# Four compressed rows between the rows of a pair, low parts on VectorE, and fewer rows scaled on ScalarE

## The chip, the core and the metric

The kernel runs on one core of a Trainium2 chip. The metric is the device time of one execution in microseconds, the median of several runs. The core has TensorE (matrix products, with its own queue for weight loads), VectorE (DVE in the rows), ScalarE (ACT), GpSimd (POOL) and SyncE (SP), which issues the transfers. Each engine works through its own queue in order and waits at semaphores for the others.

## What is computed

A transformer layer on 512 rows of width 1024, in float32: a normalisation modulated by a condition vector, a projection, two kinds of attention, an output projection, a second normalisation and a gated feed-forward part with a causal convolution. The change touches only the attention. Cut to that:

```
qa, ka, va, qb, kc, vc, ksl, vsl, kw, vw, gl = split(u @ w_in)
o_a = dilated_attention(rope(qa), rope(ka), va)               # 8 heads, 3 patterns in one masked softmax
kcc, vcc = compress(kc), compress(vc)                         # 512 positions -> 31 blocks, small gelu nets
for each of 8 heads of qb (2 groups of 4):
    o = g0 * softmax(q kcc') vcc + g1 * attention over (ksl, vsl) + g2 * attention over (kw, vw)
y = concat(o_a, o_b) @ w_o
```

The gates g come from a sigmoid of gl. With 512 rows and 8 selectable blocks of 64, all blocks are selected, so the second and the third part of o are causal attention over all keys before the row.

## The kernel before

Products keep float32 accuracy by splitting: each operand is a high part, rounded to the matrix format by a ScalarE copy, and a low part, the difference, taken on VectorE or GpSimd. A product is three matmuls (`mm3`, lines 259 to 261).

The attention is a list of 76 rows, numbered from 0. A row is one head with one kind of keys and one or two query tiles of 128 positions: (0, 1), (2) or (3), three rows for a head and kind. `BH(i)` gives the twelve rows of pair i of the gated heads (two heads, two kinds of keys), `AH(j)` the six rows of pair j of the dilated ones; `cmp_row(t)` gives one of the four compressed rows: all eight heads against the 31 compressed keys for query tile t. The constant `ROWS` sets the order: pairs b0 (rows 0 to 11), b1 (12 to 23), a0, a1 (24 to 35), b2 (36 to 47), the compressed rows 'c' (48 to 51), b3 (52 to 63), a2, a3 (64 to 75).

A loop over k (line 1303 on) interleaves the steps of several rows by the string `SEQ`: in step k it emits the scores of row k+1 (TensorE, L707 and L708; L645 for a compressed row), the masking and the row minimum of row k (VectorE, L715), its exponential (ScalarE, L721), the scaling of row k-1, the transposes of row k-3 ("turn", L741), the high part (ScalarE, L760) and the low part (VectorE, L764) of what was turned, and the product with the values of row k-5 (L789). Scaling is done by VectorE's reciprocal (L726) and then, where `e['act']` is set, by a gate multiplication on VectorE (L730) and one ScalarE activation per tile (L732), and otherwise by one GpSimd instruction per tile that takes the gate as a second scalar (L736). The flag is set for rows 4 to 19 (line 1297).

Between these steps the loop calls the filling products, two, three or four per row by the row's width: the projections of the other heads, cut into 256 pieces. Their weights come in groups, `quad_chunks(i, post)`: index 0 to 3 for the values and the second query group, 4 to 7 for the pairs a0 to a3. The high parts of a chunk are made on ScalarE (L1122), the low parts on VectorE for i under 6 and on GpSimd for a2 and a3 (L1125), two instructions of 128x512 for a chunk. Behind a finished group its results are copied, rotated (`rotate`, GpSimd, L424 to L427) and split; `v_split` does the splitting of values with one ScalarE copy and two VectorE subtractions (L505, L506). Further work that is started and then called once at a time, four times a step, are the small compression nets (`hidden`: additions L519 on GpSimd, products L1160; first the keys, then the values), the reductions for the modulation (L1033, VectorE) and the folding of finished heads. A compressed row's seven VectorE steps stand at L652 to L655, L662 to L664 and its last two subtractions at L682; its scores wait for the compressed keys and values (`needing`). After the last compressed row and the last row of a pair, `after` starts `cmp_end(h)`, which adds the compressed part to the pair's sum.

A planner places the instructions: within an engine the order follows the order of emission where it can, and later work is drawn forward into gaps that the planner's own cost model sees. Its gaps need not be those of the chip.

Of the kernel before, what the change touches and what calls it, by code (L numbers as in the profile page):

```python
# [106 lines left out]
def body(ctx, tc, nc, a, out, dbg=None):  # L107
# [18 lines left out]
    PS = 2  # L126
# [27 lines left out]
    SEQ = 'mtsmawcpmmfru'  # L154
    CUTS = (512,)
    OP = (16, 8, 0)
    ROWS = ('b0', 'b1', 'a0', 'a1', 'b2', 'c', 'b3', 'a2', 'a3')
    ORDER = ('vb', 'va0', 'a0', 'a1', 'qb23', 'va1', 'a2', 'a3')
    NBP = 1
    N0P = ()  # L160
# [2 lines left out]
    CD = ()  # L163
# [3 lines left out]
    V, A, P, T = nc.vector, nc.scalar, nc.gpsimd, nc.tensor  # L167
# [23 lines left out]
    def q4(name, dt=F32, shape=(128, 1024)):  # L191
        return slot('q4', NQ, list(shape), dt, name)
# [4 lines left out]
    def wraw(shape=(128, 1024)):  # L197
        return slot('wr', NR, list(shape), F32, 'wraw')
# [4 lines left out]
    def whl(shape=(128, 1024)):  # L203
        return slot('wh', 2, list(shape), F32R, 'whi'), slot('wl', 2, list(shape), F32R, 'wlo')
# [31 lines left out]
    def f(x):  # L236
        return x.bitcast(F32)

    def load(dst, src, queue=nc.sync):
        queue.dma_start(dst, src)  # L240
# [76 lines left out]
    for t in range(NT):  # L317
# [3 lines left out]
        y = xt[t]  # L321
        ag = stats(y)
        if True:
            nb = offset_of(ag, P if NBP else V)
            cs = [slice(0, 1024)]
            if t == 3:
                cs = [slice(0, X3), slice(X3, 1024)]
                if XV:
                    c = cs.pop(0)
# [38 lines left out]
    for j in range(KD):  # L368
        if j == 0:
            ada_cols(0)  # L370
        w = wraw((128, NC1))
        load(w, a['w_first'][j])
        wh, wl = whl((128, NC1))
# [5 lines left out]
        y = xT[j]  # L379
# [49 lines left out]
    def product(w, ts, banks):  # L429

        wh, wl = w
        for t in range(NT):
            tk = slice(128 * t, 128 * t + 128)
            if len(banks) <= t // 2:
                while live[0] >= BANKS['acc']:
                    count('acc')
                    run_misc(True)
                banks.append(acc_bank('quad'))
            o_ = banks[t // 2][:, 256 * (t % 2):256 * (t % 2) + 256]
            for i, k in enumerate(ts):  # L440
                mm3(o_, uh[k][:, tk], ul[k][:, tk], wh[:, i, :], wl[:, i, :],
                    k == 0 and t % 2 == 0, k == KD - 1 and t % 2 == 1)
                yield
# [57 lines left out]
    def v_split(dst, src, n):  # L501
        s4 = src.rearrange("p (n e d) -> p n e d", e=2, d=64)
        d4 = dst.rearrange("p (n s d) -> p n s d", s=4, d=64)
        A.activation(d4[:, :, 0:4:3, :], s4, AF.Copy)
        V.tensor_sub(d4[:, :, 1, :], s4[:, :, 0, :], f(d4[:, :, 0, :]))  # L505
        V.tensor_sub(d4[:, :, 2, :], s4[:, :, 1, :], f(d4[:, :, 3, :]))  # L506


    def blocks_of(src, eng, res):
# [42 lines left out]
    for b in (1, 0):  # L552
        y = q4('yc', F32, (128, 2, 4, 64))
# [338 lines left out]
    def cmp_end(h):  # L892

        yield from acc_wait()
        pv = acc_bank('pvc')
        cmp_mm(h, pv, True)
        yield 2
        V.tensor_add(ysum[h], ysum[h], pv)
        acc_done()
        yield 1  # L900
        yield from pair_split(h)
# [170 lines left out]
    def count(x):  # L1072
        counts[x] += 1
# [4 lines left out]
    def start_misc(gen, early=False):  # L1078
        misc.insert(0 if early else len(misc), [0, gen])

    def run_misc(forced=False):

        tick[0] += 1
        for m in sorted(misc, key=lambda m: m[0]) if forced else list(misc):
            if forced or m[0] <= tick[0]:
                d = next(m[1], -1)
                if d == -1:
                    misc.remove(m)
                    continue
                if d == 'wait':  # L1090
                    m[0] = tick[0] + 1
                    continue
                m[0] = tick[0] + (d or 1)
                return
# [9 lines left out]
    def finish(post):  # L1104
        yield from post
        quads[1] += 1

    def quad_chunks(i, post):
        st = {}

        def fetch(c):
            def run():
                st['w', c] = wraw((128, 4, 256))
                load(st['w', c], a['w_quad'][i][:, 4 * c:4 * c + 4, :])
            return run

        def prep(c):
            def run():
                w = st['w', c]
                wh, wl = whl((128, 4, 256))  # L1120
                for p in range(2):
                    A.activation(wh[:, 2 * p:2 * p + 2], w[:, 2 * p:2 * p + 2], AF.Copy)  # L1122
                    yield
                for p in range(0, 4, PS):
                    (V if i < 6 else P).tensor_sub(wl[:, p:p + PS], w[:, p:p + PS], f(wh[:, p:p + PS]))  # L1125
                    yield
                st[c] = wh, wl
                yield
            return run

        def go(c):
            def run():
                while c not in st:
                    count('prep')
                    run_misc(True)
                if c == 0:
                    st['b'] = []
                    while quads[1] < quads[0] - 1:
                        count('post')
                        run_misc(True)  # L1140
                    quads[0] += 1
                yield from product(st[c], range(4 * c, 4 * c + 4), st['b'])
                if c == 1:
                    start_misc(finish(post(st['b'])))
            return run
        return [(fetch(c), prep(c), go(c)) for c in range(2)]
# [90 lines left out]
    def needing(names, e):  # L1237
        go = e['scores']

        def scores():  # L1240
            need(*names)
            go()
        return dict(e, scores=scores)

    BH = lambda h: [r for e in range(2) for typ in range(2) for r in nsa(h, e, typ)]
    AH = lambda j: [r for e in range(2) for r in a_head(j, e)]
    cmp_rows = [needing(('qb23', 'kc', 'vc'), cmp_row(t)) for t in range(NT)]

    def after(row, *hs):
        go = row['use']  # L1250

        def use():
            go()
            for h in hs:
                start_misc(cmp_end(h))
        row['use'] = use

    rows, done_b = [], []
    for r in ROWS:
        if r == 'c':  # L1260
            rows += cmp_rows
            after(rows[-1], *[h for h in done_b if h not in CD])
        else:
            i = int(r[1])
            rows += (BH if r[0] == 'b' else AH)(i)
            if r[0] == 'b':
                if 'c' in ROWS[:ROWS.index(r)] and i not in CD:
                    after(rows[-1], i)
                done_b.append(i)


    early = {}
# [21 lines left out]
        start_misc(late_steps(GAP, st_))  # L1294
    nrow = len(rows)
    for k, r in enumerate(rows):
        r['act'] = 4 <= k < 20
    rows[0]['scores']()
    wo_started = [False]
    wo_fill = wo_first()  # L1300
# [210 lines left out]
    def down_weights(k, hi, lo):  # L1511
        w = wraw()
        load(w, a['w_down'][k])
        P.tensor_mul(w, w, g2)  # L1514
        return w
# [11 lines left out]
    for k in range(KF - NL):  # L1527
        w = down_weights(k, None, None)
        wh, wl = whl()
# [8 lines left out]
    for t in range(NT):  # L1538
# [3 lines left out]
        for c0, c1 in zip(edges, edges[1:]):  # L1542
            h, cs = c0 // 512, slice(c0 % 512, (c1 - 1) % 512 + 1)
# [18 lines left out]
```

## Time and profile before

| what | value |
| --- | --- |
| median of three runs | 721.15 us (719.63 to 722.5) |
| the profiled execution | 724.09 us, span 722.3 us, mean granted clock 0.988 |
| TensorE busy | 692.0 us, 96% of the span |
| VectorE busy | 459.2 us, 64% |
| ScalarE busy | 347.3 us, 48% |
| GpSimd busy | 238.7 us, 33% |

In busy times of a stretch the number in brackets is how many instructions started there. The granted clock is a share of TensorE's full 2.4 GHz. In a timeline the first number is the start, the second the time taken, and a bracket at the end is the engine's idle time just before, with the instruction that ended it. A row's state tile `sa__` carries a running number, so the same number on VectorE, ScalarE and GpSimd is the same row (`sa__1128` is row 4, `sa__2478` row 31, `sa__2520` row 32, `sa__2706` row 37).

### The profile page before, as it was taken

The page shows a single profiled execution, that of the slowest core. Times are in us where ns is not written, and L with a number is a line of the kernel's source. Part 1 is how long each engine was busy: PE and PEld are TensorE (multiplying, and loading weights), DVE is VectorE, ACT ScalarE, POOL GpSimd, SP SyncE. Part 2 cuts the span into 40 slices and gives each one's busy share as a digit, 9 for nine tenths or more (in the row PEclk, how much of TensorE's full clock was granted, in tenths as well). Part 3 has the DMA queues.
Part 4 walks back from the last instruction along what each step waited for, and adds up shares of the span by engine and source line. Part 5 has one row for each costly group of instructions (what it writes and reads, how often), then busy time and mean ns, then how long its engine had stood idle before and what let it go on. Part 6 is the DMA issues. An engine that isn't in the chain of part 4 may idle for free.

```text
span 722.3 us, 10901 instructions
## 1 busy us (share of the span) xinstructions
PE 692.0 (96%) x3964; PEld 598.6 (83%) x3964; DVE 459.2 (64%) x965; ACT 347.3 (48%) x706; POOL 238.7 (33%) x252
## 2 busy tenths in 40 slices
PE   8999899899989998999999999999999999999995
PEld 7999689897889886778898888888888788888884
DVE  7879877767886989978844444554543363445236
ACT  5657487744567588916553333333433341232101
POOL 2002510342466484512310110111110355765326
PEclk8999999999999999999999999999999999999999
DMA  9967741256451212350112233444423233434002
GB/s 343 386 207 197 208 144 68 59 204 234 146 204 60 59 61 87 130 192 1 59 59 88 88 100 133 142 147 148 146 91 114 88 110 123 139 123 136 10 15 102
DMA packets 31069, 93.07 MB, mean 129 GB/s; under 512 B 4132, under 2 KB 4900, under 8 KB 31016
## 3 DMA queue, kind: packets, MB, share of 16 engines
q1 hardware_dynamic: 30580, 92.20, 37.8%
q8 instruction: 31, 0.51, 0.3%
q10 hardware_dynamic: 436, 0.18, 0.1%
q14 instruction: 22, 0.18, 0.1%
HBM read 87.13 MB, written 2.10 MB: 124 GB/s over the span
## 4 chain that ended last, share of the span: by engine, by line
PE 75%; DVE 11%; ACT 5%; POOL 3%; issue 3%; DMA 2%; POOLq 0%; SPq 0%; DVEq 0%; ACTq 0%
PE d L261 6%; PE d L260 6%; PE d L259 6%; PE pvv L259 5%; PE pvv L261 5%; PE pvv L260 5%; PE pg L259 5%; PE pg L261 5%; PE pg L260 5%; PE first L393 3%; PE quad L259 3%; PE quad L260 2%; PE quad L261 2%; PE pT L741 2%; PE hid L1160 2%
## 5 line engine op out<-in xcount | busy, mean ns | idle before, releaser
L256 DVE TENSOR_TENSOR wlo<-wraw,whi 128x1024 fp32r<-128x1024 f32 x60 | 83.7, 1395 | 122.6 <-ACT whi L255 121.4
L255 ACT ACTIVATE whi<-wraw 128x1024 fp32r<-128x1024 f32 x60 | 63.6, 1060 | 139.9 <-PE pg L260 68.1
L259 PE MATMUL quad<-whi,u 128*128 128x256 f32 x256 | 75.8, 296 | 1.0 <-DVE qo L471 1.0
L260 PE MATMUL quad<-wlo,u 128*128 128x256 f32 x256 | 73.1, 286 | 0.0
L261 PE MATMUL quad<-whi,u 128*128 128x256 f32 x256 | 73.0, 285 | 0.0
L1514 POOL TENSOR_TENSOR wraw<-wraw,arow 128x1024 f32<-128x1024 f32 x22 | 58.9, 2688 | 37.0 <-DMA wraw<-w_down 35.8
L259 PE MATMUL pg<-u,whi 128*128 128x512 f32 (+1 forms) x176 | 67.7, 385 | 0.0
L260 PE MATMUL pg<-u,whi 128*128 128x512 f32 (+1 forms) x176 | 66.8, 380 | 0.0
L261 PE MATMUL pg<-u,wlo 128*128 128x512 f32 (+1 forms) x176 | 66.8, 379 | 0.0
L261 PE MATMUL pvv<-u,wlo 128*128 128x512 f32 (+1 forms) x176 | 66.8, 379 | 0.0
L259 PE MATMUL pvv<-u,whi 128*128 128x512 f32 (+1 forms) x176 | 66.8, 379 | 0.0
L260 PE MATMUL pvv<-u,whi 128*128 128x512 f32 (+1 forms) x176 | 66.8, 379 | 0.0
L256 POOL TENSOR_TENSOR hl<-cv,hh 128x512 fp32r<-128x512 f32 x14 | 23.8, 1704 | 110.6 <-ACT hh L255 110.6
L259 PEld LDWEIGHTS quad<-whi,u 128*128 128x128 f32 x256 | 49.5, 193 | 5.8 <-issue 3.9
L260 PEld LDWEIGHTS quad<-wlo,u 128*128 128x128 f32 x256 | 49.5, 193 | 1.1 <-issue 0.4
L715 DVE CUSTOM_DVE_ANT_0 p<-sp,masks 128x128 f32<-128x128 f32 (+1 forms) x96 | 44.6, 482 | 8.6 <-PE sp L708 8.2
L261 PEld LDWEIGHTS quad<-whi,u 128*128 128x128 f32 x256 | 49.5, 193 | 0.1
L741 PE MATMUL pT<-ident,p 128*128 128x128 f32 x240 | 39.9, 280 | 7.4 <-POOL p L736 4.1
L260 PEld LDWEIGHTS pg<-u,whi 128*128 128x128 f32 x176 | 33.1, 188 | 6.7 <-issue 0.5
L259 PEld LDWEIGHTS pg<-u,whi 128*128 128x128 f32 x176 | 33.1, 188 | 6.5 <-issue 0.5
L261 PEld LDWEIGHTS pg<-u,wlo 128*128 128x128 f32 x176 | 33.1, 188 | 6.3
L260 PEld LDWEIGHTS pvv<-u,whi 128*128 128x128 f32 x176 | 33.1, 188 | 6.2
(650 smaller groups left out, 1855.3 us busy)
## 6 DMA issues: line engine op xcount, KB each, us to landing
wraw<-w_up SPq DMA_DIRECT2D x44, 512.0 KB, 3.2
wraw<-w_down SPq DMA_DIRECT2D x22, 512.0 KB, 3.3
ada<-ada_col SPq DMA_DIRECT2D x32, 256.0 KB, 5.8
wraw<-w_quad SPq DMA_DIRECT2D x16, 512.0 KB, 4.3
wraw<-ada_col SPq DMA_DIRECT2D x16, 512.0 KB, 4.3
wraw<-ada_row SPq DMA_DIRECT2D x16, 512.0 KB, 3.3
x<-x SPq DMA_DIRECT2D x8, 512.0 KB, 4.9
wraw<-w_o SPq DMA_DIRECT2D x8, 512.0 KB, 3.2
```

The source lines that it names most:

```text
L255: A.activation(hi, raw, AF.Copy)
L256: lo_engine.tensor_sub(lo, raw, f(hi))
L259: T.matmul(o_, sh, mh, start=start, stop=False)
L260: T.matmul(o_, sh, ml, start=False, stop=False)
L261: T.matmul(o_, sl, mh, start=False, stop=stop)
L393: T.matmul(o_, l[:, tk], r[:, cs], start=(j == 0 and t % 2 == 0 and x == 0 and term is terms[0]), stop=(j == KD - 1 and t % 2 == 1 and x = ...
L715: V.tensor_tensor_reduce(p[:, cols[i]], e['s'][:, cols[i]], masks[:, m0:mask0 + 512], 1.0, 3e38, op0=ALU.add, op1=ALU.min, accum_out=m_[:, ...
L741: T.transpose(e['t'][:, 128 * j:128 * j + 128], e['p'][:, 128 * j:128 * j + 128], ident)
L1160: T.matmul(acc[0:62, 0:256], bl[l_ // 8][:, l_ % 8, :], w[:, l, :], start=l_ == 0, stop=l_ == 15)
L1514: P.tensor_mul(w, w, g2)
```

## The change

The compressed rows no longer stand as a block behind pair b2. One is put behind each of its groups of three rows, so that in the new numbering they are rows 39, 43, 47 and 51, and b2 takes the others from 36 to 50; from row 52 on nothing moves. `cmp_end` of b0, b1 and b2 still starts after the last compressed row. The low parts of the weight groups a2 and a3 are taken on VectorE like the others (eight instructions). The flag for scaling on ScalarE is set for rows 12 to 19 only; rows 4 to 11, all of pair b0, are scaled on GpSimd. `v_split` makes its two subtractions in one instruction over both halves (it is called twelve times).

```
-    ROWS = ('b0', 'b1', 'a0', 'a1', 'b2', 'c', 'b3', 'a2', 'a3')
+    ROWS = ('b0', 'b1', 'a0', 'a1', 'b2', 'b3', 'a2', 'a3')
+    AT = (('b2', 2), ('b2', 5), ('b2', 8), ('b2', 11))
...
-        V.tensor_sub(d4[:, :, 1, :], s4[:, :, 0, :], f(d4[:, :, 0, :]))
-        V.tensor_sub(d4[:, :, 2, :], s4[:, :, 1, :], f(d4[:, :, 3, :]))
+        V.tensor_sub(d4[:, :, 1:3, :], s4, f(d4[:, :, 0:4:3, :]))
...
-                    (V if i < 6 else P).tensor_sub(wl[:, p:p + PS], w[:, p:p + PS], f(wh[:, p:p + PS]))
+                    V.tensor_sub(wl[:, p:p + PS], w[:, p:p + PS], f(wh[:, p:p + PS]))
...
-    rows, done_b = [], []
+    rows, last = [], {}
     for r in ROWS:
-        if r == 'c':
-            rows += cmp_rows
-            after(rows[-1], *[h for h in done_b if h not in CD])
-        else:
-            i = int(r[1])
-            rows += (BH if r[0] == 'b' else AH)(i)
-            if r[0] == 'b':
-                if 'c' in ROWS[:ROWS.index(r)] and i not in CD:
-                    after(rows[-1], i)
-                done_b.append(i)
+        i = int(r[1])
+        new = (BH if r[0] == 'b' else AH)(i)
+        for n_, row in enumerate(new):
+            rows.append(row)
+            if (r, n_) in AT:
+                rows.append(cmp_rows[AT.index((r, n_))])
+        if r[0] == 'b':
+            last[i] = new[-1]
+    for i, row in last.items():
+        after(max(row, cmp_rows[-1], key=lambda x: [y is x for y in rows].index(True)), i)
...
-        r['act'] = 4 <= k < 20
+        r['act'] = 12 <= k < 20
```

## Rows read from the trace of the kernel before

**Rows 1.** The page's first part: busy us, share of the span, instructions.
```profile
PE 692.0 (96%) x3964; PEld 598.6 (83%) x3964; DVE 459.2 (64%) x965; ACT 347.3 (48%) x706; POOL 238.7 (33%) x252
```

**Rows 2.** Busy us by stretch; behind the engines the granted clock, DMA share, GB/s.
```profile
80.00:100.00 20.00, 17.57 (x118) 14.31 (x118) 17.45 (x57) 13.79 (x37) 10.41 (x11) 1.00 0.62 210
100.00:120.00 20.00, 20.00 (x143) 16.95 (x142) 13.31 (x48) 15.57 (x42) 0.00 (x0) 1.00 0.26 86
200.00:220.00 20.00, 17.68 (x134) 17.36 (x134) 16.71 (x55) 12.90 (x36) 14.30 (x17) 0.91 0.54 191
212.00:252.00 40.00, 38.47 (x320) 37.51 (x319) 31.75 (x98) 26.73 (x70) 23.46 (x35) 1.00 0.23 75
220.00:240.00 20.00, 20.00 (x169) 19.76 (x168) 13.00 (x39) 13.98 (x36) 12.84 (x21) 1.00 0.08 30
240.00:260.00 20.00, 18.47 (x145) 17.34 (x144) 19.45 (x64) 13.45 (x39) 8.47 (x12) 1.00 0.21 55
```

**Rows 3.** Timeline of TensorE: three waits (start, us taken, instruction, idle before).
```profile
90.50 0.55 PE L741 MATMUL pT<-ident,p 128*128 128x128 f32 x3 [1.08 <-ACT p L732]
...
203.33 0.89 PE L741 MATMUL pT<-ident,p 128*128 128x128 f32 x4 [2.32 <-POOL p L736]
...
247.75 0.39 PE L259 MATMUL quad<-whi,u 128*128 128x256 f32 x1 [1.00 <-DVE qo L471]
```

**Rows 4.** Timeline of GpSimd, 195 to 205 us.
```profile
195.99 2.14 POOL L736 TENSOR_SCALAR p<-p,sa__2478 128x384 f32<-128x384 f32 x1 [0.36 <-DVE sa__2478 L726]
198.13 3.51 POOL L1125 TENSOR_TENSOR wlo<-wraw,whi 128x512 fp32r<-128x512 f32 x2
201.61 1.66 POOL L736 TENSOR_SCALAR p<-p,sa__2520 128x512 f32<-128x512 f32 x1
...
204.05 0.59 POOL L736 TENSOR_SCALAR p<-p,sa__2594 128x384 f32<-128x384 f32 x1
```

**Rows 5.** Busy us by stretch as in rows 2, around the wait for GpSimd.
```profile
202.00:204.00 2.00, 0.67 (x5) 0.68 (x5) 1.97 (x7) 0.36 (x2) 2.00 (x3) 0.90 0.66 217
204.00:206.00 2.00, 2.00 (x12) 2.00 (x11) 1.72 (x3) 0.60 (x1) 0.64 (x2) 0.50 0.91 334
206.00:208.00 2.00, 2.00 (x14) 2.00 (x14) 1.33 (x6) 0.97 (x3) 0.00 (x0) 0.74 0.69 250
```

**Rows 6.** Line 1125: ns shortest/median/longest, first and last start in us.
```profile
L1125 DVE TENSOR_TENSOR wlo<-wraw,whi x24: 628/688/989, 52.9 to 180.9; 128x512 fp32r<-128x512 f32 x24
...
L1125 POOL TENSOR_TENSOR wlo<-wraw,whi x8: 1269/1288/2262, 198.1 to 240.7; 128x512 fp32r<-128x512 f32 x8
```

**Rows 7.** Timelines of GpSimd, VectorE and ScalarE around row 4.
```profile
84.83 8.84 POOL L519 TENSOR_TENSOR bst<-vct,cin 64x248 f32<-64x248 f32 x8
...
87.19 0.15 DVE L726 RECIPROCAL sa__1128<-sa__1128 128x1 f32<-128x1 f32 x1
...
89.06 0.68 DVE L730 TENSOR_TENSOR sa__1128<-sa__1128,gates 128x1 f32<-128x1 f32 x1
...
89.83 0.62 ACT L732 ACTIVATE p<-p,sa__1128 128x384 f32<-128x384 f32 x1 [1.31 <-DVE sa__1128 L730]
```

**Rows 8.** Timeline of GpSimd: scaling with a gate (x2 is one wide row).
```profile
212.09 0.98 POOL L736 TENSOR_SCALAR p<-p,sa__2677,gates 128x128 f32<-128x128 f32 x2
213.72 0.66 POOL L736 TENSOR_SCALAR p<-p,sa__2706,gates 128x384 f32<-128x384 f32 x1 [0.65 <-PE quad L261]
...
217.46 0.77 POOL L736 TENSOR_SCALAR p<-p,sa__2744,gates 128x512 f32<-128x512 f32 x1
```

**Rows 9.** Single tiles (columns as in rows 6): compressed scores, their masking, compressed values, split values.
```profile
L645 PE MATMUL sc<-kcs,qe x16: 276/277/278, 234.5 to 243.7; 128*128 128x64 f32 x16
...
L652 DVE TENSOR_TENSOR pc<-sc,cmask x4: 407/414/415, 236.2 to 245.9; 128x256 f32<-128x256 f32 x4
...
L625 DVE TENSOR_TENSOR vp<-vcp,vp x1: 272/272/272, 183.6 to 183.6; 128x128 fp32r<-128x128 f32 x1
...
L505 DVE TENSOR_TENSOR va<-quad,va x8: 266/284/292, 94.4 to 218.5; 128x128 fp32r<-128x128 f32 x8
```

## Prediction

> **What bounds the kernel now.** I read the page's busy times first. TensorE is busy for 96% of the span [rows 1], so what any edit can give back is TensorE's idle time and its time at a lower clock, some 30 us of the span in all, and only where the edit stands. Next come the busy times in stretches of 20 us; the edits lie between 60 and 260 us. The reader is to compare VectorE with TensorE there: from 220 to 240 us TensorE is full and VectorE has 7 us of 20 free, from 240 to 260 us VectorE is busy for 19.45 of 20 and TensorE loses 1.53 us, from 80 to 100 us it loses 2.43 us beside a VectorE at 17.45, and from 200 to 220 us it loses 2.32 us and the granted clock is 0.91 [rows 2]. Then the timeline of TensorE, where a bracket gives each wait and who ended it. Three matter: 1.08 us until ScalarE had scaled a row, 2.32 us until GpSimd had, and 1.00 us for VectorE where the compressed rows stood in a block [rows 3]. Last, the timelines of the engines that ended these waits.
>
> **The low parts of the last two weight groups (the main gain).** GpSimd's queue runs in order. At 195.99 it scales row 31, then it makes two low parts, 3.51 us, and only at 201.61 does it scale row 32 [rows 4]. TensorE turns row 32 and waits for it for 2.32 us [rows 3]. After that wait the granted clock falls: 0.90, 0.50 and 0.74 in the three stretches from 202 to 208 us [rows 5]; 0.50 is 1.2 instead of 2.4 GHz. The shortfalls, 0.10, 0.50 and 0.26 of 2 us each, come to an estimate of 1.72 us of work lost. The two low parts thus cost 2.32 + 1.72 = 4.04 us, and that is the upper end of the gain. The other six come later, the last at 240.7 [rows 6], and no wait of TensorE for GpSimd stands in that stretch (full from 220 to 240 us [rows 2]); taking them off GpSimd gives nothing.
>
> What VectorE gets: eight low parts at 0.69 us instead of 1.29 us on GpSimd [rows 6], 5.5 us of work. Two of them come where VectorE is busy for 1.97 of 2 us [rows 5], so they delay what stands behind them by up to 1.38 us: the reciprocals of rows 33 and 34, then GpSimd's scaling, then TensorE's transposes. Between none of it reaching TensorE and all of it I take half, 0.7 us, as a row is turned two steps after it is scaled. Net: 4.04 - 0.7 = 3.3 us less (ends 4.04 and, with the whole delay and half of the clock loss left, 1.8).
>
> GpSimd and VectorE do slow each other: a 128x384 scaling took 2.14 us at 195.99, while VectorE ran its long reductions, and 0.59 us at 204.05 [rows 4]. The Trainium skill (SBUF — State Buffer, Who interferes with whom) says that a VectorE instruction with two SBUF inputs and a GpSimd instruction that reads SBUF exclude each other for a whole instruction, whichever starts first. That speaks against this change, for a low part is such an instruction, and more rows are to be scaled on GpSimd; the rows of 2.14 and 0.59 us agree. What it would make of the time is the third rival.
>
> **Rows 4 to 11 scaled on GpSimd.** These are the last eight of the first pair's twelve rows. ScalarE loses one activation or two per row (0.62 us for a 128x384 tile), VectorE loses eight multiplications by the gate. Row 4 shows what that is worth: its reciprocal is made at 87.19, but the multiplication comes only at 89.06, takes 0.68 us, and ScalarE scales at 89.83 [rows 7]; TensorE has waited 1.08 us then [rows 3]. GpSimd takes the gate as a second scalar, so it needs the reciprocal alone, and costs 0.66 us for such a tile, 0.77 for 128x512 and 0.98 for the two tiles of a wide row [rows 8]: 3 x 0.66 + 3 x 0.77 + 2 x 0.98 = 6.3 us over the 20 us in which the eight rows run. GpSimd has the room (busy for 10.41 of 20 us, then for none [rows 2]). In its queue stands a block of eight additions, 84.83 to 93.67, 1.1 us each [rows 7]. TensorE wants row 4 at 89.42 (90.50 less the wait). If the scaling follows the third addition, at 88.15, it ends at 88.8, in time; behind the fourth it ends at 89.9. The additions belong to a later step of the program, so I take it that the scaling goes before most of them: 1.1 us less (ends: 1.1 less, 3.8 us more before any fall of the clock). From 100 to 120 us TensorE is full with ScalarE busy for 15.57 of 20 us [rows 2], so rows 9 to 11 change nothing.
>
> **The four compressed rows.** Each has seven steps on VectorE, five of them on a 128x256 tile like the masking of 0.41 us, and two subtractions of 128x128 like the 0.28 us of the split values [rows 9]; with the small ones an estimate of 3 us a row. Now they stand at rows 48 to 51; after the change at 39, 43, 47 and 51, so the first one's scores move from 234.5 us [rows 9] to the step that scales row 37, 213.72 [rows 8]. They wait for the compressed values, whose last part is written at 183.6 us [rows 9]: no wait is added there, and no weight products are pulled forward. The number of filling products per row stays, so the fill ends at the same row. What goes is the wait of 1.00 us [rows 3] and what is small beside it, all of the 1.53 us that TensorE loses from 212 to 252 us [rows 2]. What may come: in these 40 us VectorE is busy for 31.75 us [rows 2]; with six more low parts (4.1 us) it is 35.9 of the 38.5 us that TensorE needs, 93%. At 65 and 67% TensorE lost nothing, at 87% 2.43 of 20 us, at 97% 1.53 [rows 2]. If 2.43 of 20 hold over 38.5 us, 4.7 us are lost, 3.1 more than now. Evenly spread rows are easier to hide than a block, but the load is higher; I take 0 (ends 1.5 less, 3.1 more).
>
> **The merged subtraction.** Twelve times two instructions of 0.28 us, started 0.2 us apart, become one of the size that costs 0.41 us [rows 9]: a tenth of a microsecond or less each, beside a TensorE that waits for none of them. 0.
>
> **Sum.** -3.3 - 1.1 + 0 = -4.4 us. The profiled execution was 724.09 us (span 722.3), so its like would be 719.7; the median of the runs is 721.15, 2.9 lower, and gives 716.8. A change of under 0.5%, 3.6 us, is about what a measurement here cannot tell from none.
>
> **The rivals.** First: VectorE becomes the bound from 200 to 252 us. The compressed rows then cost 3.1 us: -3.3 - 1.1 + 3.1 = -1.3, 719.9 us. For it speaks the 93%, against it that TensorE has filling products in all of that stretch. Second, slower than before: the scaling of row 4 stands behind all eight additions. It ends at 93.67 + 0.66 = 94.3, TensorE waits 4.9 instead of 1.08 us, 3.8 more, and as the wait of 2.32 us was followed by the low clock, 1.7 more: +5.5 - 3.3 = +2.2, 723.4 us. It decides from the fourth addition on. For it speaks that the block now runs without a gap, against it that the additions are wanted later. Third, the exclusion of GpSimd and VectorE: row 32 waits for two low parts of 0.69 us on the other engine, 1.38 of the 2.32 us stays with half the clock loss, so the main gain is 1.8; rows 4 to 11 gain nothing, for each tile may take 2.14 instead of 0.66 us: -1.8, 719.4 us. The rule of the Trainium skill cited above would act in this way. That the change does not act at all I rule out: instructions change engine.
>
> **How the numbers follow.** Forecast 0.58, first rival 0.20, second 0.12, third 0.07, others 0.03. The forecast's own range is 714.3 (all gains at their ends) to 719. The range takes in the first and third rival and reaches towards the second: 713.8 to 722.5. Faster by over 0.5% means under 717.5: some seven tenths of the forecast and a part of the rest, 0.43. Slower by over 0.5% means over 724.7: part of the second rival and of a worse first one, 0.12. Between them 0.45.
>
> **What would show it.** Right, if near 200 us TensorE no longer waits for GpSimd and the granted clock there is 1.00; if rows 4 to 6 are turned without a wait; if TensorE is idle for at most 1.5 us in the 40 us that hold the compressed rows. Wrong, if a new wait for GpSimd stands near 90 us, if waits for VectorE of about 1 us appear at every compressed row, or if a fall of the clock turns up at another place. The order in which each engine gets its instructions is set by a planner that sees the moved work too, so places beside the edits can shift by a microsecond or two either way.

## The result and the profile after

The changed kernel takes 716.1 us in the median of thirteen runs (714.99 to 719.98), the kernel before 721.15 us in thirteen runs beside them (719.44 to 725.26). The ratio is 0.9938 with a 95% interval of 0.9923 to 0.9954: 4.5 us less, between 3.3 and 5.6. On another chip, in a later comparison, the ratio of the same two kernels was 0.9947 (0.9927 to 0.9966), 3.8 us. The forecast was 716.8 us, 4.4 us less. The profiled execution took 718.01 us, span 716.2; that of before had 724.09 and 722.3.

The page of the changed kernel, busy times (answers to [rows 1]) and the granted clock in 40 slices of the span, in tenths:

```profile
PE 690.0 (96%) x3964; PEld 596.9 (83%) x3964; DVE 458.7 (64%) x953; ACT 343.6 (48%) x696; POOL 234.5 (33%) x254
...
PEclk8999999999999999999999999999999999999998
```

TensorE has the same 3964 products; the 6.1 us by which the span is shorter are idle time and time at a low clock. Busy times by stretch of the changed kernel, columns as in [rows 2]:

```profile
80.00:100.00 20.00, 20.00 (x135) 16.31 (x135) 15.64 (x46) 12.14 (x34) 8.24 (x12) 1.00 0.56 193
100.00:120.00 20.00, 20.00 (x152) 17.82 (x150) 13.94 (x48) 14.71 (x39) 6.62 (x9) 1.00 0.32 107
200.00:220.00 20.00, 18.45 (x147) 17.45 (x146) 18.45 (x58) 13.35 (x37) 10.02 (x13) 1.00 0.47 160
205.00:245.00 40.00, 38.66 (x317) 37.61 (x317) 35.86 (x115) 28.80 (x81) 19.30 (x31) 1.00 0.24 82
240.00:260.00 20.00, 19.49 (x150) 18.06 (x148) 17.48 (x53) 16.14 (x43) 10.03 (x17) 1.00 0.34 96
```

From 80 to 100 us TensorE is now full where it lost 2.43 us; from 200 to 220 us the clock is 1.00 instead of 0.91; from 240 to 260 us it loses 0.51 instead of 1.53 us [rows 2]. VectorE has become busier in the stretch of the compressed rows: 35.86 of the 40 us from 205 to 245, and TensorE still loses only 1.34 us there.

The waits of TensorE at the places of [rows 3], and one ahead of them at 182.75 that both kernels have (timeline of TensorE, changed kernel):

```profile
182.75 0.48 PE L463 MATMUL qT<-ident,yq 128*128 128x128 f32 x1 [1.47 <-POOL yq L428]
...
201.67 0.44 PE L741 MATMUL pT<-ident,p 128*128 128x128 f32 x2 [0.56 <-POOL p L736]
207.50 0.66 PE L741 MATMUL pT<-ident,p 128*128 128x128 f32 x4 [0.80 <-POOL p L736]
...
243.01 0.63 PE L463 MATMUL qT<-ident,yq 128*128 128x128 f32 x4 [0.51 <-DVE qo L472]
```

The wait of 1.08 us for ScalarE is gone without a successor. The one of 2.32 us for GpSimd has two small ones in its place, 0.56 and 0.80 us, and the 1.00 us for VectorE is 0.51. What stands before the two small ones is seen in the timelines of GpSimd and VectorE of the changed kernel (`sa__1124` is row 4, `sa__2431` row 30, `sa__2462`, `sa__2504`, `sa__2541` are rows 31 to 33, and `sa__2620` is row 35):

```profile
85.68 0.66 POOL L736 TENSOR_SCALAR p<-p,sa__1124,gates 128x384 f32<-128x384 f32 x1 [2.46 <-DVE sa__1124 L726]
...
192.09 0.82 POOL L736 TENSOR_SCALAR p<-p,sa__2431 128x128 f32<-128x128 f32 x2 [9.39 <-DVE sa__2431 L726]
193.28 2.13 POOL L736 TENSOR_SCALAR p<-p,sa__2462 128x384 f32<-128x384 f32 x1 [0.37 <-DVE sa__2462 L726]
196.29 1.65 POOL L736 TENSOR_SCALAR p<-p,sa__2504 128x512 f32<-128x512 f32 x1 [0.88 <-DVE sa__2504 L726]
198.57 3.04 POOL L736 TENSOR_SCALAR p<-p,sa__2541 128x128 f32<-128x128 f32 x2 [0.63 <-DVE sa__2541 L726]
...
203.94 1.81 POOL L844 TENSOR_TENSOR ol<-fold,oh 128x512 fp32r<-128x512 f32 x1 [1.24 <-ACT oh L842]
205.73 1.71 POOL L736 TENSOR_SCALAR p<-p,sa__2620 128x512 f32<-128x512 f32 x1
...
198.25 0.15 DVE L726 RECIPROCAL sa__2541<-sa__2541 128x2 f32<-128x2 f32 x1
198.33 0.66 DVE L1125 TENSOR_TENSOR wlo<-wraw,whi 128x512 fp32r<-128x512 f32 x1
198.92 1.27 DVE L1033 CUSTOM_DVE_ANT_0 wraw<-wraw,crow,b_col 128x1024 f32<-128x1024 f32 x1
200.13 0.54 DVE L764 TENSOR_TENSOR pTl<-pT,pTh 128x384 fp32r<-128x384 f32 x1
...
205.60 1.28 DVE L1033 CUSTOM_DVE_ANT_0 wraw<-wraw,crow,b_col 128x1024 f32<-128x1024 f32 x1
```

Row 32 is scaled straight behind row 31, at 196.29 instead of 201.61 [rows 4]. But row 33 takes 3.04 us for two tiles of 128x128, where row 30 took 0.82 for the same two: VectorE runs the low part, a reduction and another subtraction in just that time. The Trainium skill (SBUF — State Buffer, Who interferes with whom) says that such a VectorE instruction, with two inputs from SBUF, and a GpSimd instruction that reads SBUF exclude each other for a whole instruction; the rows of 0.82 and 3.04 us agree.

The second small wait has no low part beside it. Row 35's reciprocal is made at 205.07 us, but GpSimd is still in a subtraction for finished heads (L844) until 205.73, and its scaling then takes 1.71 us beside a reduction on VectorE. In the kernel before, the same subtraction stands ahead of row 35 too, and the scaling behind it took 0.69 us, at 211.41.

Read along the span, the two traces come apart in steps. The scaling of row 31 starts at 193.28 instead of 195.99 [rows 4], 2.7 us earlier; at the end the span is 6.1 us shorter. Of the 2.7 us, 1.6 are there by row 2, ahead of rows 4 to 11: its scaling starts at 79.95 instead of 81.59 us; the other 1.1 are the wait of 1.08 us that is gone. The 3.4 us behind row 31 belong to the low parts and the compressed rows. One pair of executions gives 6.1 us where the runs give 4.5 (by the ratio) to 5.0 (by the medians); how much each part is worth is for the experiments.

### The profile page after: what moved, and what is told of

Read it like the earlier page. It is cut to its first block, busy times and chain, and to the rows that moved or that the text cites. A ratio compares the mean times of both kernels' runs of the same rounds, so it can differ in the third digit from the quotient of the medians.

```text
span 716.2 us, 10890 instructions
## 1 busy us (share of the span) xinstructions
PE 690.0 (96%) x3964; PEld 596.9 (83%) x3964; DVE 458.7 (64%) x953; ACT 343.6 (48%) x696; POOL 234.5 (33%) x254
## 4 chain that ended last, share of the span: by engine, by line
PE 77%; DVE 11%; ACT 5%; issue 3%; POOL 2%; DMA 2%; POOLq 0%; SPq 0%; DVEq 0%; ACTq 0%
PE d L260 6%; PE d L262 6%; PE d L261 6%; PE pvv L261 5%; PE pvv L260 5%; PE pvv L262 5%; PE pg L261 5%; PE pg L260 5%; PE pg L262 5%; PE first L394 3%; PE quad L260 3%; PE quad L261 2%; PE quad L262 2%; PE pT L741 2%; PE hid L1160 2%
## 5 line engine op out<-in xcount | busy, mean ns | idle before, releaser
L257 DVE TENSOR_TENSOR wlo<-wraw,whi 128x1024 fp32r<-128x1024 f32 x60 | 85.9, 1431 | 125.4 <-ACT whi L256 124.2
L262 PEld LDWEIGHTS pvv<-u,wlo 128*128 128x128 f32 x176 | 33.1, 188 | 6.2
```

Source lines behind the costliest of these rows:

```text
L257: lo_engine.tensor_sub(lo, raw, f(hi))
L262: T.matmul(o_, sl, mh, start=False, stop=stop)
```

## The experiments

The theory: the parts add, each at its own place in the span. Its rivals are those of the prediction, part by part. First each part alone in the kernel before, four kernels on one chip, where the kernel before took 722.08 us; then each part taken out of the changed kernel, four on another chip, with the kernel before at 722.56 us. All times are medians, and a gain is worked out as the ratio's distance from 1 times 721.15 us. An interval of a ratio is 1.1 to 1.6 us to either side, and a difference of two ratios carries some 1.7 us (an estimate). The changed kernel was not run beside the second four; its ratio of 0.9938 is from another chip, and with the later 0.9947 each of their differences to it is 0.6 us lower.

**The merged subtraction alone.**

```
-        V.tensor_sub(d4[:, :, 1, :], s4[:, :, 0, :], f(d4[:, :, 0, :]))
-        V.tensor_sub(d4[:, :, 2, :], s4[:, :, 1, :], f(d4[:, :, 3, :]))
+        V.tensor_sub(d4[:, :, 1:3, :], s4, f(d4[:, :, 0:4:3, :]))
```

> The kernel before with the merged subtraction alone. Theory of parts (each part gives its time at its own place, and the parts add up): the two traces are 1.65 us apart by row 2's scaling, before any other part acts; if that is the merged subtraction, by letting the mask of row 3 go ahead of a reduction that waits for its transfer, this kernel is 1 to 1.6 us below before. Rival (the early shift is the landing of one transfer, which differs from execution to execution): within 0.4 us of before, as predicted.

Measured: 722.08 us, ratio 0.9991 (0.9973 to 1.0008), 0.6 us less with an interval from 1.9 less to 0.6 more. No difference can be told, as the prediction forecast, and the interval holds both what the theory and what the rival expected. The trace shows more. Row 2 is scaled at 79.63 us. Over all profiles of this study that start lies between 79.45 and 81.12 us in the eight with the merged subtraction (mean 80.1), between 80.47 and 82.60 in the six without (mean 81.6). What differs is an order on VectorE (timeline of VectorE, the kernel before and then the changed one; `sa__1095` and `sa__1091` are row 3):

```profile
77.67 1.29 DVE L1033 CUSTOM_DVE_ANT_0 wraw<-wraw,crow,b_col 128x1024 f32<-128x1024 f32 x1 [2.87 <-DMA wraw<-ada_col]
...
79.08 0.28 DVE L715 CUSTOM_DVE_ANT_0 p<-sp,masks 128x128 f32<-128x128 f32 x1
```

```profile
74.78 0.29 DVE L715 CUSTOM_DVE_ANT_0 p<-sp,masks 128x128 f32<-128x128 f32 x1
...
76.50 1.28 DVE L1033 CUSTOM_DVE_ANT_0 wraw<-wraw,crow,b_col 128x1024 f32<-128x1024 f32 x1 [1.42 <-DMA wraw<-ada_col]
```

With the subtraction merged, the first mask of row 3 stands ahead of a reduction that waits for weights, not behind it. The subtraction itself saves little (one of 0.41 us for two of 0.28, started 0.2 us apart); the place of a neighbour is better. The second thing is the clock. TensorE's wait for GpSimd is there as in the kernel before, and the clock does something else (timeline of TensorE, then busy times by stretch, this kernel):

```profile
201.06 0.66 PE L740 MATMUL pT<-ident,p 128*128 128x128 f32 x4 [2.31 <-POOL p L735]
...
200.00:202.00 2.00, 0.94 (x8) 0.94 (x9) 1.97 (x7) 0.35 (x3) 2.00 (x4) 1.00 0.72 256
202.00:204.00 2.00, 2.00 (x19) 2.00 (x18) 1.94 (x3) 1.06 (x3) 0.37 (x1) 1.00 0.78 313
```

The same wait, 2.31 us, at the same instruction, and the granted clock stays at 1.00, where the kernel before fell to 0.50 [rows 5]. The low clock behind this wait is not a fixed cost. Nor is it saved in this execution: the clock falls later, to 0.86, 0.50 and 0.79 in the three stretches from 274 to 280 us, where the kernel before has no fall, and 1.70 us of work are lost there.

**The low parts alone.**

```
-                    (V if i < 6 else P).tensor_sub(wl[:, p:p + PS], w[:, p:p + PS], f(wh[:, p:p + PS]))
+                    V.tensor_sub(wl[:, p:p + PS], w[:, p:p + PS], f(wh[:, p:p + PS]))
```

> The kernel before with the low parts of the last two weight groups on VectorE, nothing else. Theory of parts: no wait of over 1 us for GpSimd near 201 us and a granted clock of 1.00 there; 1.8 to 3.3 us below before. Rival (the gain is of the whole, the planner's new order, and not of one place): within 1 us of before although the wait is gone.

Measured: 719.83 us, ratio 0.9970 (0.9954 to 0.9986), 2.2 us less (1.0 to 3.3). The wait of 2.32 us is gone, and the two of 0.55 and 0.79 us are there as in the changed kernel. The granted clocks of the runs tell how often the fall had come: their mean is 0.9914 in these twelve runs and 0.9895 in the 35 of the kernel before. A fall that loses 1.7 us takes 0.0024 off the mean of a run of 720 us, so these runs have some 0.8 falls fewer each (an estimate).

**Rows 4 to 11 on GpSimd alone.**

```
-        r['act'] = 4 <= k < 20
+        r['act'] = 12 <= k < 20
```

> The kernel before with rows 4 to 11 scaled on GpSimd, nothing else. Theory of parts: the wait of 1.08 us near 90 us is gone and no other comes; 0.8 to 1.3 us below before. Rival from the prediction (the scaling stands behind the block of eight additions): 2 to 5 us above before, with a wait for GpSimd near 90 us.

Measured: 721.07 us, ratio 0.9988 (0.9970 to 1.0005), 0.9 us less, with an interval that reaches past zero. In its trace the wait of 1.08 us for ScalarE near 90 us is gone, and no other stands between 84 and 96 us.

**The compressed rows spread, alone.** The edit is that of the row list in the diff of the change.

> The kernel before with the four compressed rows between the rows of the third pair, nothing else. Theory of parts: VectorE is less full here than in the changed kernel, as the low parts stay on GpSimd; 0.5 to 1.5 us below before. Rival (VectorE becomes the bound beside spread rows): 1 us or more above before, waits for VectorE at each compressed row.

Measured: 722.54 us, ratio 1.0002 (0.9982 to 1.0021): no difference. In its trace TensorE waits 0.30 us at 223.71 and 0.60 us at 249.07 in the stretch of the compressed rows; the kernel before has 1.00 us [rows 3] and two waits of 0.29 and 0.25 us behind it. So 0.6 us are gained there, less than this comparison can tell from nothing. The clock takes it back: the mean over the twelve runs is 0.9871 against 0.9895, one fall more in a run by the same estimate. In the profile it stands from 278 to 284 us (0.86, 0.50 and 0.79), where the kernel before has none.

**The changed kernel with the subtraction in two instructions.** The edit of the first experiment, backwards.

> The changed kernel with the two subtractions of the split values put back. Parts that add up (single parts were 0.6, 2.2, 0.9 us below before and the compressed rows at 0): 0.6 us above the changed kernel, 3.9 below before. Rival (the parts need each other): 2 us or more above the changed kernel.

Measured: 716.73 us, ratio to the kernel before 0.9932 (0.9916 to 0.9948), no worse than the changed kernel's 0.9938, though row 2 is scaled at 81.36 us here, 1.4 us later. So of the earlier start that the merged subtraction gives row 2, no part is seen in the time, here or alone.

**The changed kernel with the low parts back on GpSimd.**

> The changed kernel with the low parts of the last two weight groups back on GpSimd. Parts that add up: 2.2 us above the changed kernel, 2.3 below before, with the wait for GpSimd near 198 us and the low clock back. Rival (the parts need each other): all of the gain is gone, within 1 us of before.

Measured: 719.64 us, ratio 0.9965 (0.9947 to 0.9983), 2.0 us more than the changed kernel's ratio gives. That all of the gain is gone, as the rival had it, lies outside the interval. The wait is back and here the clock falls behind it (timeline of TensorE, then stretches, this kernel):

```profile
200.25 0.85 PE L741 MATMUL pT<-ident,p 128*128 128x128 f32 x4 [2.31 <-POOL p L736]
...
200.00:202.00 2.00, 1.75 (x10) 1.75 (x11) 1.73 (x6) 0.60 (x1) 1.56 (x4) 0.65 0.92 371
202.00:204.00 2.00, 2.00 (x11) 2.00 (x11) 2.00 (x6) 0.09 (x1) 0.00 (x0) 0.50 0.87 344
```

**The changed kernel with rows 4 to 11 on ScalarE.**

> The changed kernel with rows 4 to 11 scaled on ScalarE again. Parts that add up: 0.9 us above the changed kernel, 3.6 below before. Rival (the parts need each other): 2 us or more above the changed kernel.

Measured: 718.71 us, ratio 0.9953 (0.9935 to 0.9971), 1.1 us more than the changed kernel's, which with its doubt excludes neither 0 nor the rival's 2 us. The wait for ScalarE is back at row 4, at 87.85 us, with 0.46 us. Its size goes with how soon behind row 4's reciprocal TensorE gets there: 2.2 us behind it in the kernel before (87.19 to 89.42 us), which waits 1.08 us, and 2.9 us here (84.54 to 87.39). In the six profiles in which ScalarE scales row 4 the wait is 0.39 to 1.17 us, 0.8 on average.

**The changed kernel with the compressed rows in a block.**

> The changed kernel with the compressed rows as a block behind the third pair again. Parts that add up: the time of the changed kernel within 0.5 us, since spreading alone gave nothing. Rival (the low parts on VectorE make the block costly, so spreading pays only beside them): 1 to 2 us above the changed kernel, with waits for VectorE inside the block.

Measured: 719.02 us, ratio 0.9957 (0.9940 to 0.9973), 1.4 us more: what the rival expected, and not the theory's 0.5. With the low parts on VectorE the block has a wait for GpSimd that it did not have before (timelines of TensorE, GpSimd and VectorE, this kernel; its line numbers are one lower than the changed kernel's):

```profile
235.64 0.44 PE L462 MATMUL qT<-ident,yq 128*128 128x128 f32 x2 [0.72 <-POOL yq L427]
...
243.71 0.41 PE L706 MATMUL sp<-khh,qe 128*128 128x384 f32 x1 [0.27 <-DVE pc L652]
246.51 0.44 PE L671 MATMUL pcT<-ident,pc 128*128 128x128 f32 x2 [0.25 <-POOL pc L666]
...
233.55 0.77 POOL L425 TENSOR_TENSOR rt<-yq,rope 128x64 f32<-128x64 f32 x1
234.29 0.76 POOL L426 TENSOR_TENSOR rt<-yq,rope 128x64 f32<-128x64 f32 x1
...
233.21 1.66 DVE L1124 TENSOR_TENSOR wlo<-wraw,whi 128x512 fp32r<-128x512 f32 x2
```

The rotation's products on GpSimd take 0.77 and 0.76 us beside two low parts on VectorE (0.33 us for one of this size at 231.86 in the same trace), and TensorE waits 0.72 us for the rotation. Its waits in the stretch come to 0.72 + 0.27 + 0.25 = 1.24 us, against 0.51 in the changed kernel: 0.7 us of the 1.4 are seen in waits. The kernel with the low parts alone, which has the block too, shows the same three waits (0.71, 0.27 and 0.24 us). In sum they are not more than what the block costs with the low parts on GpSimd, 1.00 + 0.29 + 0.25 = 1.54 us.

**One row of scaling instead of eight low parts.** If the low parts cost what they did by standing ahead of row 32 in GpSimd's queue, then taking that one row off the queue must do as much, with every low part left where it was. The kernel before, with row 32 scaled on ScalarE:

```
-        r['act'] = 4 <= k < 20
+        r['act'] = 4 <= k < 20 or k == 32
```

> The kernel before, with one row more (row 32) scaled on ScalarE; all low parts stay where they were, on GpSimd for the last two weight groups. If GpSimd's order in its queue is what cost the 2 us that the low parts are worth, row 32 no longer stands behind two low parts of 3.5 us, the wait of 2.3 us of TensorE near 201 us is gone or below 0.6 us, and the time is 1.5 to 2.5 us below the kernel before. If it is the work that VectorE and GpSimd share (load, not order), taking one scaling away changes little: within 1 us of the kernel before.

Measured, on a third chip with the kernel before at 720.94 us: 718.86 us, ratio 0.9967 (0.9952 to 0.9982), 2.4 us less by the ratio. No wait of TensorE of 0.3 us or more stands between 185 and 244 us, although GpSimd does as much beside VectorE as before (timelines of GpSimd and ScalarE, this kernel):

```profile
195.15 2.13 POOL L736 TENSOR_SCALAR p<-p,sa__2478 128x384 f32<-128x384 f32 x1 [0.37 <-DVE sa__2478 L726]
197.29 3.51 POOL L1125 TENSOR_TENSOR wlo<-wraw,whi 128x512 fp32r<-128x512 f32 x2
200.78 1.79 POOL L736 TENSOR_SCALAR p<-p,sa__2557 128x128 f32<-128x128 f32 x2
...
198.53 0.72 ACT L732 ACTIVATE p<-p,sa__2520 128x512 f32<-128x512 f32 x1
```

The low parts still take 3.51 us, but row 32 (`sa__2520`) no longer stands behind them, so its place in that queue was enough to make the wait. That load had no part in it is not shown: in the kernel before, the two low parts and row 32 took 3.51 + 1.66 us beside VectorE [rows 4], where the shortest low part on GpSimd takes 1.27 us [rows 6] and a scaling of that size 0.69 at 211.41. At those prices row 32 would have been done 1.9 us sooner (an estimate). The mean clock of these twelve runs is 0.9916 against 0.9896 in the 18 of the kernel before beside them, 0.8 falls fewer here too.

**The wait at 182.75.** It is the largest that the changed kernel has left near the edits. Two kernels try to take it and the two small ones away; the changed kernel itself runs beside them on the third chip, 717.82 us, ratio 0.9947 (0.9927 to 0.9966). First the rotation behind pair a1 on VectorE:

```
-                ys.append(evac_half(banks[b], b, 2, P))
+                ys.append(evac_half(banks[b], b, 2, V if j == 1 else P))
```

> The changed kernel, with the rotation behind the second pair of the dilated heads on VectorE instead of GpSimd. In the changed kernel TensorE waits 1.47 us for GpSimd's last addition of that rotation at 182.75 us, and the clock is at 0.5 for some 3 us behind it in most profiles. If parts add each at its place: the wait falls under 0.5 us and the time is 1 to 2.5 us below the changed kernel (the wait alone, up to the wait and 1.5 us of clock). If VectorE is the bound there (16.9 of 20 us busy from 180 to 200 us), the wait moves to VectorE and the time is within 0.5 us of the changed kernel.

> The changed kernel itself, on the same chip as the three others, as their reference: some 4.5 us below the kernel before (3.3 to 5.6).

Measured: 716.94 us, ratio 0.9942 (0.9922 to 0.9962), which its reference's interval covers. The edit missed its mark: the rotations that it moves stand at 148 and 156 us; the one behind the wait belongs to another group and stayed on GpSimd. The wait went all the same, and another came ahead of it (timelines of TensorE, ScalarE and VectorE; the changed kernel on this chip first, then the edited one):

```profile
174.60 1.02 PE L1043 MATMUL gr<-arow,ones 128*128 128x512 f32 x2
177.27 0.66 PE L463 MATMUL qT<-ident,yq 128*128 128x128 f32 x4 [0.56 <-ACT arow L1045]
...
176.62 0.60 ACT L1045 ACTIVATE arow<-gr 128x512 f32<-128x512 f32 x1
...
171.14 1.28 DVE L1024 SCALAR_TENSOR_TENSOR arow<-wraw,ccol,arow 128x1024 f32<-128x1024 f32 x1 [1.65 <-DMA wraw<-ada_row]
```

```profile
173.22 1.02 PE L1043 MATMUL gr<-arow,ones 128*128 128x512 f32 x2
177.11 0.74 PE L463 MATMUL qT<-ident,yq 128*128 128x128 f32 x4 [1.79 <-ACT arow L1045]
...
176.46 0.60 ACT L1045 ACTIVATE arow<-gr 128x512 f32<-128x512 f32 x1
...
171.24 1.29 DVE L1024 SCALAR_TENSOR_TENSOR arow<-wraw,ccol,arow 128x1024 f32<-128x1024 f32 x1 [2.35 <-DMA wraw<-ada_row]
```

TensorE comes to this place 1.4 us earlier (173.22 against 174.60), but VectorE gets the modulation's weights at 171.24 against 171.14 us, and ScalarE's copy, which stands behind the steps that follow on it, starts at 176.46 against 176.62. The 1.4 us are given back as wait: 1.79 instead of 0.56 us. In this pair of traces, what is gained ahead of the transfer does not pass it. That is no rule of this place: from the kernel before to the changed one the same step of VectorE moved from 173.48 to 170.83 us, and TensorE's lead of 2.65 us near 135 us (137.73 and 135.08) was 2.70 at 177 us (179.95 and 177.25). At the end the edited kernel's span is 1.5 us shorter than its reference's (714.7 and 716.2), and 1.0 of it stands at 134.39 against 135.40 us, ahead of all that the edit moves. The 0.5 us that are left agree with the times.

Then rows 31 to 35 on ScalarE as well:

```
-        r['act'] = 12 <= k < 20
+        r['act'] = 12 <= k < 20 or 31 <= k < 36
```

> As the one before, and rows 31 to 35 scaled on ScalarE besides. The changed kernel has two more waits for GpSimd's scaling there, 0.56 at 201.67 and 0.80 at 207.50 us. If parts add: 0.8 to 1.4 us below the kernel with the rotation on VectorE, 2 to 3.5 us below the changed kernel. If ScalarE or VectorE (one multiplication more for gated rows, none here) becomes the last one there: same as the kernel with the rotation alone, within 0.5 us.

Measured: 716.99 us, ratio 0.9937 (0.9915 to 0.9959): the same as the kernel with the rotation alone, though both small waits for GpSimd are gone from its trace, and the stretch from row 30's scaling to a wait near 270 us, which the next paragraph looks at, is 1.3 us shorter (73.30 against 74.62). The mean clock of its six runs is 0.9897, that of the other six 0.9918: 0.9 falls more in a run would take back the gain, but six runs each leave that in doubt. The three kernels on this chip can't be told apart, so none is shown to beat the changed one.

**The stretch that holds the low parts and the compressed rows.** In every profile GpSimd scales row 30 behind an idle time of 7 us or more, and near 270 us TensorE waits 1.34 to 1.40 us for VectorE's low part of a turned row. Between these two marks lie all low parts and compressed rows of the change. Behind the second mark eleven of the fourteen profiles take 449.4 to 449.9 us to the end of the span, and the three in which the clock falls near 275 us take 451.0 to 451.1. So what a trace gains ahead of the second mark is kept, but for such a fall. Busy us by stretch as in [rows 2], the stretch in one piece; the kernel before, the subtraction alone, the low parts alone, row 32 on ScalarE, the compressed rows alone, the changed kernel:

```profile
194.79:272.79 78.00, 72.74 (x558) 68.66 (x557) 65.29 (x192) 54.70 (x146) 51.72 (x68) 0.98 0.29 97
192.53:269.06 76.53, 71.25 (x559) 67.15 (x557) 64.96 (x188) 54.69 (x146) 51.66 (x68) 1.00 0.30 99
192.61:269.03 76.42, 72.07 (x558) 67.00 (x557) 68.51 (x200) 54.84 (x146) 44.54 (x60) 1.00 0.30 95
193.96:269.15 75.19, 71.91 (x558) 67.28 (x558) 64.83 (x192) 55.38 (x147) 51.77 (x67) 1.00 0.31 101
195.69:272.81 77.12, 72.40 (x559) 68.61 (x557) 65.85 (x192) 55.03 (x146) 51.52 (x68) 0.98 0.31 99
192.09:266.75 74.66, 71.23 (x559) 67.07 (x557) 67.35 (x196) 55.29 (x146) 43.84 (x60) 1.00 0.31 102
```

The two at 0.98 hold the fall near 204 us. Less its 1.7 us the kernel before takes 76.3 us, near the 76.5 of the subtraction alone, which has the same waits and no fall. The low parts alone take 76.4 (76.0 in the changed kernel with the block), so without the fall they are worth 0.6 us at the most there, and 0.4 to 0.8 us beside the spread rows. Row 32 on ScalarE takes 75.2, 1.1 to 1.3 us less. The compressed rows take 75.4 without the fall (75.1 in the changed kernel with the low parts back), 0.9 to 1.5 us less, and beside the low parts the spread is worth 1.3 to 1.8 us (76.0 and 76.4 against 74.7).

## Why the prediction was right

**The low parts (3.3 us forecast).** The place was right: the wait and the fall of the clock near 200 us are gone, and one moved row does the same. The size was too high: 2.2 us alone and 2.0 by undoing it, inside the stated ends of 1.8 and 4.04. The terms of the sum were off.

The first is the clock, 1.72 us taken as certain. Five profiles have the wait of 2.31 or 2.32 us: the kernel before, the ones with the subtraction alone, rows 4 to 11 alone, and the compressed rows alone, and the changed one with the low parts put back. In four the clock falls behind it and 1.70 to 1.72 us of work are lost; in the one with the subtraction alone it falls at a later place. On average that is some 1.4 us, and the 0.8 falls by which the runs' mean clocks differ give the same.

The second is the wait with its delay, 2.32 - 0.7 = 1.6 us. With the fall taken out, the stretch between the two marks shows 0.6 us at the most for the low parts alone. Two waits, 0.56 + 0.80 = 1.36 us, stand where the wait was, twice the 0.7 that I took for the delay. And TensorE's busy time in the stretch rises from 71.0 us (72.74 less the fall) or 71.25 to 72.07 with the low parts alone; why is open. The 1.4 us of clock and up to 0.6 us of wait come near to the 2.2 and 2.0 measured. By these figures most of the gain is the fall of the clock that comes less often, where the forecast had put as much on the wait.

The road of the delay was not the one described either. I read VectorE's load from 202 to 204 us, but the two low parts stood at 198 to 202, and I let them hold up the reciprocal of row 33. That came in time, at 198.25; GpSimd's scaling itself ran 3.04 instead of 0.82 us beside VectorE. That is the third rival's mechanism: it acts, on row 33 and with 0.56 us of wait, not at the price of the whole gain. The 0.80 us at row 35 has no term in the prediction.

**Rows 4 to 11 (1.1 us forecast).** 0.9 us alone, 1.1 by undoing it, and neither is clear of the interval. By the traces, from row 2's scaling to TensorE's wait near 135 us the six profiles with these rows on ScalarE take 55.4 to 56.1 us, the eight with them on GpSimd 54.8 to 55.1, on average 0.9 us less. The 1.08 us were taken from one trace of a wait that is 0.8 us on average. Row 4's scaling takes 0.66 us, the duration taken from [rows 8], and starts at 85.68 us, 0.3 us behind its reciprocal. The choice on which the second rival hung came out as chosen and by more than was needed: the planner put all eight additions behind pair b0, the first at 102.17 us, so none stands ahead of a scaling.

**The compressed rows (0 forecast, ends 1.5 less and 3.1 more).** VectorE's load is as worked out, 35.86 us in 40 against 35.9 in 38.5, and the first rival did not come: at 90% VectorE TensorE waits 0.51 us for it in that stretch. What came is the gain end: 0.9 to 1.5 us alone and 1.3 to 1.8 beside the low parts between the two marks, of which the waits are 0.6 and 0.7. The times are 0 and 1.4. That the spread alone shows no time goes with the fall near 280 us in its profile and with the low mean clock of its runs; why falls come more often there is open. Whether the spread is worth more beside the low parts stays open too: by the waits it is not, and the intervals of the two times are as wide as their difference.

**The merged subtraction (0).** By the times 0: 0.6 us less alone, 0.4 us less when it is undone, both within the intervals. By the traces row 2 starts 1.4 us earlier on average, by a shift of the kind that the prediction's last sentence allows for. No trace shows it given back behind row 2, so it is either a part of the times that the intervals hide, or chance in row 2's start, which differs by up to 2.1 us between profiles of one order. These runs can't tell.

**The sum.** -4.4 us forecast, -4.5 measured (-3.8 in the later comparison). That it came out so closely is luck: the low parts gave about 1.2 us less than forecast, the compressed rows up to 1.4 more. The parts alone add to 0.6 + 2.2 + 0.9 - 0.1 = 3.6 us, the parts taken out to -0.4 + 2.0 + 1.1 + 1.4 = 4.1, or to 1.4 with the changed kernel's later ratio, whose doubt counts four times in that sum. So the times don't contradict that the parts add and don't show it; that each acts at its own place is what the traces show. Two figures of the prediction are put wrongly: the end of the forecast's own range is 721.15 - 6.64 = 714.5, not 714.3, and the some 30 us of the first paragraph are idle time alone (722.3 - 692.0), to which the time at a lower clock comes on top.

Of the signs named ahead, rows 4 to 6 without a wait, no new wait near 90 us, at most 1.5 us of idle time at the compressed rows (1.34), no 1 us waits there the clock of 1.00 near 200 us and no fall at a new place came as said. "TensorE no longer waits for GpSimd" did not: 1.36 us of such waits are left.

## What to carry to other kernels

Where an engine's queue runs in order, look at what stands ahead of the instruction that the bottleneck waits for: one row moved out of GpSimd's queue gave what eight moved low parts gave (2.4 and 2.2 us). Work moved from GpSimd to VectorE is priced twice, in VectorE's time and in what GpSimd's next instructions take beside it. A wait in a trace is not yet what its removal gives: here 2.32 us of wait came to 0.6 us or less, and 0.6 us of waits at the compressed rows to 0.9 or more. Compare a stretch that starts ahead of the wait and ends at the same instruction behind it. A fall of the clock that one trace shows behind a wait is weighed by how often it comes, and the mean clocks of many runs tell that where one trace can't. Whether a gain passes a late transfer depends on whether the transfer comes earlier with it.

## What the runs showed of the hardware

That the same wait is followed by a low clock in some executions and not in others was not expected. The wait of 1.47 us for GpSimd near 183 us stands in twelve of the profiles; behind nine of them the clock falls, behind three it stays at 1.00. The fall in the changed kernel (stretches of 2 us):

```profile
182.00:184.00 2.00, 1.25 (x6) 1.25 (x7) 1.64 (x4) 0.55 (x2) 0.70 (x1) 0.69 0.80 168
184.00:186.00 2.00, 2.00 (x11) 2.00 (x10) 1.28 (x2) 0.66 (x2) 0.00 (x0) 0.50 1.03 306
186.00:188.00 2.00, 2.00 (x17) 2.00 (x17) 0.40 (x4) 0.00 (x0) 0.00 (x0) 0.96 0.76 261
```

The shortfalls, 0.31, 0.50 and 0.04 of 2 us each, are 1.70 us again: the fall, where it comes, costs nearly the same whether the wait ahead was 1.47 or 2.32 us. So a longer wait did not make a dearer fall, and the length of the wait did not decide whether one came. What decides it is not shown by these runs. A third place says the same: near 270 us all fourteen profiles have a wait of 1.34 to 1.40 us for VectorE and, some 4 us behind it, one of 0.47 to 0.49 us for GpSimd, and in three of them (the subtraction alone, the compressed rows alone, and the changed kernel with the block) the clock falls some 2 us behind the second.
